# Norm stages in column halves, output stored in halves, and sixteen matmuls on a zeroed tile at the beginning

## The chip, the cores and the metric

The kernel runs on one core of a Trainium2 chip. The core has a matmul engine (TensorE, PE in the profile; its weight loads are listed apart as PEld), a vector engine (VectorE, DVE), an activation engine (ScalarE, ACT), a general engine (GpSimd, POOL) and a queue engine (SyncE, SP) that issues the DMA transfers here. Each engine works through its own list of instructions in order, and an instruction waits where it needs what another engine or a transfer has not finished. The metric is the time of one execution on the device in microseconds (us).

## The reference

The kernel computes four layers over 256 tokens of width 1024. Each layer is a half-step SwiGLU feed-forward network (FFN, inner width 2816), a token mixer with attention to 256 memory rows, and a second FFN. Each of the three takes a normed x and adds its normed result to x:

```python
def rms_norm(x, g):
    xf = x.astype(jnp.float32)
    y = xf * lax.rsqrt(jnp.mean(xf * xf, axis=-1, keepdims=True) + RMS_EPS)
    return (y * g.astype(jnp.float32)).astype(x.dtype)

def swiglu_ffn(x, w_gate_up, w_down):
    gate, up = jnp.split(x @ w_gate_up, 2, axis=-1)
    return (jax.nn.silu(gate) * up) @ w_down

for i in range(DEPTH):          # DEPTH = 4
    kind, j = i % 3, i // 3
    g = norm_g[i]
    x = x + 0.5 * rms_norm(swiglu_ffn(rms_norm(x, g[0]), ffn_w_gate_up[i, 0], ffn_w_down[i, 0]), g[1])
    h = rms_norm(x, g[2])
    mem_n = rms_norm(mem, mem_norm_g[i])
    y = ...                     # mixer A, B, C, A in layers 0 to 3, ends in a product with w_out
    x = x + rms_norm(y, g[3])
    x = x + 0.5 * rms_norm(swiglu_ffn(rms_norm(x, g[4]), ffn_w_gate_up[i, 1], ffn_w_down[i, 1]), g[5])
```

Between two of these parts stands what is called a norm boundary below: the result y of one part is normed and added to x, and x is normed for the next part. There are eleven such inner boundaries, one opening (only the norm of the input) and one end (only the norm of y, the addition and the store).

## The kernel before

**Layout.** x stays on the chip as two tiles (t = 0 and t = 1) of 128 tokens on partitions by 1024 columns, in float32. For the next part's matmuls the normed rows are transposed by TensorE in eight 128x128 blocks per tile, four to a PSUM tile of 512 columns (`rot`, four buffers).

**Three passes.** Every float32 product is made of three matmuls of operands split into a high and a low part (`mm3`, lines 334 to 336: hi by hi, hi by lo, lo by hi). A split is two instructions (`split`, lines 309 and 310): ScalarE copies the tile rounded into `hi`, VectorE subtracts that from the tile into `lo`. The weights stream in by SyncE's queue as units of 128x1024 (`raw`, five buffers) and are split into a ring of ten `hi` and `lo` buffers. A ring buffer comes free when TensorE has done the last matmul that reads it, and so ScalarE's `hi` can wait for TensorE. The same two lines split the transposed activations (`xth`, `xtl`); line 404 keeps a plain copy (`xf`) where an FFN follows, which works on two of its six column sets with a scheme of seven products in place of eight.

**A boundary.** `ln_stages` writes four stages for each tile t. s1: ScalarE squares the part's result in PSUM (`acc`, 128x1024) with the sum over columns as a by-product (line 374); VectorE multiplies the same result by the gain into `rows` (375); GpSimd makes 1/sqrt of the sum (348 adds epsilon, 349 takes the power). s2: VectorE adds rows times that factor to x (379). s3: ScalarE squares x (382), GpSimd as before. s4: VectorE makes the normed rows (386). `turn(t)` runs the four, `trans(t)` the eight transposes (400) with their splits.

**Order.** The two tiles are staggered. The last part's matmuls go tile 0 first (in `ffn`, `down(j, 0, ...)`, line 691 of the profile; in a mixer `out_step` with line 954). `turn(0)` follows, and TensorE meanwhile goes on with tile 1's matmuls; `trans(0)` stands inside the last but one of these (`late`, lines 747 and 961; after mixer B, ahead of all of them). Then comes `turn(1)`, and `trans(1)` inside the first products of the next part (line 584 in an FFN), or in the mixer's own beginning. Between these the calls of `slot` let the weight splits and loads of later units in. So the source gives an order; the framework's tile scheduler then merges all instructions, by its own estimates, into the list of each engine, and puts in the waits. In the program that results, weight splits of later units stand between the stages of a boundary, on ScalarE and on VectorE.

**Beginning and end.** `setup` loads x, the gain and the first five weight units, runs `turn(0)`, `trans(0)`, `turn(1)` and lets the weight splits begin; `first_set` of the first FFN is the first user. At the end, after the last `turn(1)`, two stores of 512 KB write x (line 753).

Of the kernel before, what the change touches and what calls it, by code (L numbers as in the profile page):

```python
# [18 lines left out]
P = 128  # L19
# [13 lines left out]
RING = 10  # L33
RAW = 5
HELD = 8
GRP = 4

def pairs(*cols):
# [165 lines left out]
class Trunk:  # L204
# [153 lines left out]
    def ln_stages(self, st, t, ps, post_scale, post_eps, gpost, gpre):  # L358
        nc = self.nc
        if "rows" not in st:  # L360
            st["rows"] = None
        ss = self.small.tile([P, 1], F32, tag="ss", name="ss", bufs=8)
        r = self.small.tile([P, 1], F32, tag="r", name="r", bufs=8)
        ss2 = self.small.tile([P, 1], F32, tag="ss2", name="ss2", bufs=8)
        r2 = self.small.tile([P, 1], F32, tag="r2", name="r2")
        x = self.x[t]

        def rows():
            if st["rows"] is None:
                st["rows"] = self.main.tile([P, 2, D], F32, tag="rows", name="rows")  # L370
            return st["rows"][:, t, :]

        def s1():
            nc.scalar.activation(out=self.dump(), in_=ps, func=AF.Square, scale=post_scale, accum_out=ss)  # L374
            nc.vector.tensor_tensor(out=rows(), in0=ps, in1=gpost, op=ALU.mult)  # L375
            self.rsqrt(r, ss, post_eps)

        def s2():
            nc.vector.scalar_tensor_tensor(out=x, in0=rows(), scalar=r, in1=x, op0=ALU.mult, op1=ALU.add)  # L379

        def s3():
            nc.scalar.activation(out=self.dump(), in_=x, func=AF.Square, scale=1 / 32, accum_out=ss2)
            self.rsqrt(r2, ss2, self.eps1)

        def s4():
            nc.vector.scalar_tensor_tensor(out=rows(), in0=x, scalar=r2, in1=gpre, op0=ALU.mult, op1=ALU.mult)

        out = []
        if ps is not None:
            out += [s1, s2]  # L390
        if gpre is not None:
            out += [s3, s4]
        return out
# [36 lines left out]
    def setup(self):  # L430
# [14 lines left out]
        nc.gpsimd.memset(self.neghalf, -0.5)  # L445
        nc.gpsimd.memset(self.eps1, EPS)
        nc.gpsimd.memset(self.eps16, 16 * EPS)
        turn = self.boundary(None, None, self.gpre)
        turn(0)
        self.trans(0, keep=self.keep)  # L450
# [83 lines left out]
    def ffn(self, l, f, post_next, pre_next, last=False):  # L534
        nc, tc = self.nc, self.tc
        with tc.tile_pool(name=f"ffn{l}{f}", bufs=1, reuse_waits="tile") as fp:
# [211 lines left out]
                down(j, 1, held[j - nd], (lambda: self.trans(0, keep=self.keep if f else None)) if late else None)  # L748
                self.slot(1)
            turn(1)  # L750
        if last:
            for t in range(2):
                nc.sync.dma_start(out=self.io["out"][t * P:(t + 1) * P, :], in_=self.x[t])

    def mem_chunk(self, k):
        m = self.main.tile([P, SEQ], F32, tag="snap", name="memraw", bufs=4)
# [585 lines left out]
```

## Time and profile before

| what | value |
|---|---|
| median of three runs | 1881.27 us (1877.97 to 1881.93) |
| profiled execution, its own time | 1876.93 us |
| span of that execution in the trace | 1875.1 us |
| TensorE busy (matmuls) | 1855.1 us, 99% of the span, 9406 instructions |
| TensorE weight loads, beside the matmuls | 1550.2 us, 83% |
| VectorE | 1517.5 us, 81% |
| ScalarE | 1092.6 us, 58% |
| GpSimd | 67.7 us, 4% |
| read from HBM | 359.95 MB, 193 GB/s over the span |

A row of a timeline reads: start in us from the beginning of the span, length in us, engine, line of the kernel, operation, what is written from what with their shapes, the count of instructions in the row (x8: eight in a row, and the length is of all of them together), and in brackets how long the engine had been idle before and what released it. Matmuls overlap, so one of 128x512 is listed with 0.39 us while the next starts after 0.227. Lines are those of the kernel before the change.

### The profile page before, as it was taken

How to read it: one execution, taken by the hardware profiler on the slowest of the kernel's cores; microseconds unless marked ns; L12 is line 12 of the kernel's file. 1: busy time of each engine (PE TensorE's matmuls, PEld its weight loads, DVE VectorE, ACT ScalarE, POOL GpSimd, SP SyncE). 2: the span in 40 equal slices, each digit the busy share in tenths (PEclk: the TensorE clock that was granted, in tenths of full speed). 3: DMA queues.
4: the chain of work that ended last, by engine and by line, in shares of the span. 5: the costliest groups of instructions: out<-in, count | busy, mean ns of one | idle time of the engine just before them, and what ended most of it. 6: DMA issues, size and time to landing. Idle time of an engine off the chain costs nothing.

```text
span 1875.1 us, 25124 instructions
## 1 busy us (share of the span) xinstructions
PE 1855.1 (99%) x9406; PEld 1550.2 (83%) x9406; DVE 1517.5 (81%) x1828; ACT 1092.6 (58%) x1471; POOL 67.7 (4%) x115
## 2 busy tenths in 40 slices
PE   8999999999999999999999999999999999999998
PEld 6888988888888897888888889888888888988886
DVE  7897879886888768888688876888868897878884
ACT  7556655755566555665556556465556555655652
POOL 0000200000000100000000000000000000200000
PEclk9999999999999999999999999999999999999999
DMA  8646737645574652664557366275477436737731
GB/s 321 237 154 212 261 124 257 232 161 193 177 247 135 215 198 91 247 226 155 191 192 247 124 205 237 91 254 173 146 246 241 167 124 210 263 124 254 243 101 60
DMA packets 103867, 362.67 MB, mean 193 GB/s; under 512 B 12084, under 2 KB 16576, under 8 KB 103616
## 3 DMA queue, kind: packets, MB, share of 16 engines
q1 hardware_dynamic: 103568, 359.47, 56.1%
q8 instruction: 74, 1.21, 0.3%
q0 software_dynamic: 176, 1.59, 0.2%
q14 instruction: 49, 0.40, 0.1%
HBM read 359.95 MB, written 1.06 MB: 193 GB/s over the span
## 4 chain that ended last, share of the span: by engine, by line
PE 88%; DVE 6%; issue 3%; ACT 1%; POOL 1%; DMA 1%; SPq 0%; ACTq 0%; DVEq 0%; POOLq 0%
PE acc L691 22%; PE rot L621 16%; PE rot L334 13%; PE rot L336 13%; PE rot L335 13%; PE acc L954 3%; DVE lo L310 3%; PE rot L562 2%; PE rot L856 1%; PE acc L874 1%; DMA raw<-in_w 1%; PE rot L888 1%; DVE x L379 1%; PE rot L400 1%; DVE rows L375 1%
## 5 line engine op out<-in xcount | busy, mean ns | idle before, releaser
L310 DVE TENSOR_TENSOR lo<-raw,hi 128x1024 fp32r<-128x1024 f32 (+1 forms) x515 | 620.2, 1220 | 142.9 <-ACT hi L309 135.2
L309 ACT ACTIVATE hi<-raw 128x1024 fp32r<-128x1024 f32 (+1 forms) x515 | 536.2, 1053 | 266.5 <-PE acc L691 84.1
L334 PE MATMUL rot<-hi,xth 128*128 128x512 f32 (+3 forms) x1072 | 415.2, 387 | 0.5 <-ACT hi L309 0.5
L336 PE MATMUL rot<-hi,xtl 128*128 128x512 f32 (+3 forms) x1072 | 412.2, 385 | 0.4 <-DVE xtl L310 0.3
L335 PE MATMUL rot<-lo,xth 128*128 128x512 f32 (+3 forms) x1072 | 411.6, 384 | 0.3 <-DVE lo L310 0.3
L309 ACT ACTIVATE hi<-quad 128x1024 fp32r<-128x1024 f32 x224 | 235.5, 1059 | 201.6 <-PE rot L336 129.2
L310 DVE TENSOR_TENSOR lo<-quad,hi 128x1024 fp32r<-128x1024 f32 x224 | 272.1, 1222 | 25.0 <-ACT hi L309 21.1
L336 PEld LDWEIGHTS rot<-hi,xtl 128*128 128x128 f32 x1072 | 201.7, 188 | 42.7 <-DVE xtl L310 4.0
L334 PEld LDWEIGHTS rot<-hi,xth 128*128 128x128 f32 x1072 | 201.8, 188 | 39.1 <-ACT hi L309 1.1
L335 PEld LDWEIGHTS rot<-lo,xth 128*128 128x128 f32 x1072 | 201.9, 188 | 38.8 <-DVE lo L310 0.7
L691 PE MATMUL acc<-hi,hh 128*128 128x512 f32 x640 | 197.9, 390 | 0.0
L691 PE MATMUL acc<-lo,hh 128*128 128x512 f32 x640 | 197.2, 389 | 0.0
L691 PE MATMUL acc<-hi,hl 128*128 128x512 f32 x640 | 197.1, 389 | 0.0
L621 PE MATMUL rot<-hi,sums 128*128 128x512 f32 x512 | 169.0, 396 | 0.1
L277 DVE TENSOR_TENSOR quad<-quad 128x1024 f32<-128x1024 f32 x128 | 154.8, 1220 | 1.2
L691 PEld LDWEIGHTS acc<-hi,hl 128*128 128x128 f32 x640 | 120.1, 188 | 25.2
L691 PEld LDWEIGHTS acc<-lo,hh 128*128 128x128 f32 x640 | 120.1, 188 | 25.1
L691 PEld LDWEIGHTS acc<-hi,hh 128*128 128x128 f32 x640 | 119.5, 188 | 24.3
L621 PEld LDWEIGHTS rot<-hi,sums 128*128 128x128 f32 x512 | 96.1, 188 | 24.3 <-DVE snap L641 4.8
L621 PE MATMUL rot<-lo,sums 128*128 128x512 f32 x256 | 99.8, 390 | 0.0
L348 POOL TENSOR_TENSOR r<-ss,thin 128x1 f32<-128x1 f32 x48 | 23.5, 490 | 1577.5 <-ACT junk L374 1484.7
L621 PE MATMUL rot<-hi,xtl 128*128 128x512 f32 x192 | 74.8, 389 | 0.0
(212 smaller groups left out, 2363.8 us busy)
## 6 DMA issues: line engine op xcount, KB each, us to landing
raw<-in_w SPq DMA_DIRECT2D x504, 512.0 KB, 4.5
quad<-in_w SPq DMA_DIRECT2D x128, 512.0 KB, 5.8
gpre<-in_norm_g SPq DMA_DIRECT2D x8, 512.0 KB, 5.6
gpost<-in_norm_g SPq DMA_DIRECT2D x8, 512.0 KB, 4.5
memraw<-in_mem_t SPq DMA_DIRECT2D x32, 128.0 KB, 4.3
g<-in_norm_g SPq DMA_DIRECT2D x8, 512.0 KB, 6.1
raw<-in_w SPq DMA_DIRECT2D x8, 384.0 KB, 3.7
sw<-in_sw SPq DMA_DIRECT2D x2, 768.0 KB, 9.0
```

The lines of the kernel that those rows point to most:

```text
L277: add = lambda x, y: self.nc.vector.tensor_tensor(out=x, in0=x, in1=y, op=ALU.add)
L309: self.nc.scalar.activation(out=hi, in_=src, func=AF.Copy)
L310: self.nc.vector.tensor_tensor(out=lo, in0=src, in1=hi.bitcast(F32), op=ALU.subtract)
L334: mm(out, a[0], b[0], start=start, stop=False)
L335: mm(out, a[0], b[1], start=False, stop=False)
L336: mm(out, a[1], b[0], start=False, stop=stop)
L348: g.tensor_tensor(out=out, in0=ss, in1=eps_tile, op=ALU.add)
L375: nc.vector.tensor_tensor(out=rows(), in0=ps, in1=gpost, op=ALU.mult)
L562: nc.tensor.transpose(ps[:, k * P:(k + 1) * P], T[s][t][:, k * P:(k + 1) * P], self.ident)
L621: nc.tensor.matmul(ps, a[i], w[j][:, kk, :], start=fresh and h == kk == i == j == 0, stop=h == kk == i == 1, skip_group_check=True)
L691: mm(ys[t][:, n * 512:(n + 1) * 512], x, y[:, 0, n * 512:(n + 1) * 512], start=(j == 0 and x is a[0] and y is w[0]), stop=(j == NF - 1 and ...
L954: self.nc.tensor.matmul(o["y"][t][:, h * 512:(h + 1) * 512], x, y[:, 0, h * 512:(h + 1) * 512], start=(j == 0 and x is a[0] and y is w[0]) ...
```

## The change

The edit is to the norm stages, to `setup` and to the stores. In s1 each tile's result is now worked on in two column halves of 512: ScalarE squares the first while VectorE multiplies the second by the gain, then each takes the other half. The two sums of squares are put together by one more addition on GpSimd. s2 is one instruction as before, but at the end of the program it is two halves, and each is stored as soon as it is there: four stores of 256 KB in place of two of 512 KB. s4 makes the normed rows in two halves, and so the first four transposes read only the first. s3 is unchanged. At the beginning VectorE zeroes a tile, and TensorE does 16 matmuls of 128x512 on it into a PSUM tile that nobody reads.

```diff
--- before.py
+++ after.py
@@ -33,6 +33,7 @@
 RING = 10
 RAW = 5
 HELD = 8
+WARM = 16
 GRP = 4
 
 def pairs(*cols):
@@ -359,11 +360,12 @@
         nc = self.nc
         if "rows" not in st:
             st["rows"] = None
-        ss = self.small.tile([P, 1], F32, tag="ss", name="ss", bufs=8)
+        ss = self.small.tile([P, 2], F32, tag="ss", name="ss", bufs=8)
         r = self.small.tile([P, 1], F32, tag="r", name="r", bufs=8)
         ss2 = self.small.tile([P, 1], F32, tag="ss2", name="ss2", bufs=8)
         r2 = self.small.tile([P, 1], F32, tag="r2", name="r2")
         x = self.x[t]
+        H = D // 2
 
         def rows():
             if st["rows"] is None:
@@ -371,19 +373,33 @@
             return st["rows"][:, t, :]
 
         def s1():
-            nc.scalar.activation(out=self.dump(), in_=ps, func=AF.Square, scale=post_scale, accum_out=ss)
-            nc.vector.tensor_tensor(out=rows(), in0=ps, in1=gpost, op=ALU.mult)
-            self.rsqrt(r, ss, post_eps)
+            dump = self.dump()
+            for a, b in ((0, 1), (1, 0)):
+                nc.scalar.activation(out=dump[:, a * H:a * H + H], in_=ps[:, a * H:a * H + H], func=AF.Square,
+                                     scale=post_scale, accum_out=ss[:, a:a + 1])
+                nc.vector.tensor_tensor(out=rows()[:, b * H:b * H + H], in0=ps[:, b * H:b * H + H],
+                                        in1=gpost[:, b * H:b * H + H], op=ALU.mult)
+            nc.gpsimd.tensor_tensor(out=r, in0=ss[:, 0:1], in1=post_eps, op=ALU.add)
+            self.rsqrt(r, ss[:, 1:2], r)
 
         def s2():
-            nc.vector.scalar_tensor_tensor(out=x, in0=rows(), scalar=r, in1=x, op0=ALU.mult, op1=ALU.add)
+            parts = 2 if gpre is None else 1
+            for i in range(parts):
+                h = slice(i * D // parts, (i + 1) * D // parts)
+                nc.vector.scalar_tensor_tensor(out=x[:, h], in0=rows()[:, h], scalar=r, in1=x[:, h], op0=ALU.mult,
+                                               op1=ALU.add)
+                if gpre is None:
+                    nc.sync.dma_start(out=self.io["out"][t * P:(t + 1) * P, h], in_=x[:, h])
 
         def s3():
             nc.scalar.activation(out=self.dump(), in_=x, func=AF.Square, scale=1 / 32, accum_out=ss2)
             self.rsqrt(r2, ss2, self.eps1)
 
         def s4():
-            nc.vector.scalar_tensor_tensor(out=rows(), in0=x, scalar=r2, in1=gpre, op0=ALU.mult, op1=ALU.mult)
+            for i in range(2):
+                h = slice(i * H, i * H + H)
+                nc.vector.scalar_tensor_tensor(out=rows()[:, h], in0=x[:, h], scalar=r2, in1=gpre[:, h], op0=ALU.mult,
+                                               op1=ALU.mult)
 
         out = []
         if ps is not None:
@@ -445,6 +461,11 @@
         nc.gpsimd.memset(self.neghalf, -0.5)
         nc.gpsimd.memset(self.eps1, EPS)
         nc.gpsimd.memset(self.eps16, 16 * EPS)
+        warm = self.dump()
+        nc.vector.memset(warm, 0.0)
+        ps = self.rot()
+        for _ in range(WARM):
+            nc.tensor.matmul(ps, warm[:, :P], warm[:, 512:], start=True, stop=True)
         turn = self.boundary(None, None, self.gpre)
         turn(0)
         self.trans(0, keep=self.keep)
@@ -748,9 +769,6 @@
                 down(j, 1, held[j - nd], (lambda: self.trans(0, keep=self.keep if f else None)) if late else None)
                 self.slot(1)
             turn(1)
-        if last:
-            for t in range(2):
-                nc.sync.dma_start(out=self.io["out"][t * P:(t + 1) * P, :], in_=self.x[t])
 
     def mem_chunk(self, k):
         m = self.main.tile([P, SEQ], F32, tag="snap", name="memraw", bufs=4)
```

In the changed kernel the lines are numbered up to 22 higher: the squares are L378 (before L374), the products L380 (L375), x is L389 (L379), its square L395 (L382), the rows L401 (L386), the transposes L416 (L400), weight splits L310 and L311 (L309 and L310), the mixer's output matmuls L972 (L954).

The merged lists of the engines differ by more than the diff says. First place: ScalarE, at the boundary out of the mixer of layer 0 into its second FFN, first tile. `acc` is the mixer's output in PSUM, `junk` a tile that nobody reads, `ss` the sum of squares, `hi` and `raw` the weight units; what stands behind "waits" is the engine or queue that the instruction waits for. Before:

```order
L374 ACTIVATE junk,ss<-acc 128x1024 [waits PE_49]
L309 ACTIVATE hi<-raw 128x1024 [waits DMAHW6_49,PE_49]
L309 ACTIVATE hi<-raw 128x1024 [waits DMAHW7_49,PE_49]
L382 ACTIVATE junk,ss_2530<-x_72 128x1024 [waits DVE_49]
L309 ACTIVATE hi<-raw 128x1024 [waits DMAHW0_49,PE_49]
```

and after the change:

```order
L378 ACTIVATE junk,ss<-acc 128x512 [waits PE_49]
L310 ACTIVATE hi<-raw 128x1024 [waits DMAHW6_49,PE_49]
L378 ACTIVATE junk,ss<-acc 128x512 [waits DVE_49]
L310 ACTIVATE hi<-raw 128x1024 [waits DMAHW7_49,PE_49]
L310 ACTIVATE hi<-raw 128x1024 [waits DMAHW0_49,PE_49]
L310 ACTIVATE hi<-raw 128x1024 [waits DMAHW2_49,PE_49]
L395 ACTIVATE junk,ss_2559<-x_72 128x1024 [waits DVE_49]
```

A weight split stands between the two squares, and four of them in place of two stand ahead of the square of x. The second square waits for VectorE.

VectorE at the same place, before:

```order
L375 TENSOR_TENSOR rows<-acc,g_1938 128x1024 [waits Activation_49]
L379 SCALAR_TENSOR_TENSOR x_72<-rows,r,x_72 128x1024 [waits DVE_49,Pool_49]
L310 TENSOR_TENSOR lo<-raw,hi 128x1024 [waits DMAHW6_49,Activation_49]
L310 TENSOR_TENSOR lo<-raw,hi 128x1024 [waits DMAHW7_49,Activation_49]
L386 SCALAR_TENSOR_TENSOR rows<-x_72,r_2531,g_1940 128x1024 [waits DVE_49,Pool_49]
```

and after the change:

```order
L380 TENSOR_TENSOR rows<-acc,g_1967 128x512 [waits Activation_49]
L311 TENSOR_TENSOR lo<-raw,hi 128x1024 [waits DMAHW6_49,Activation_49]
L380 TENSOR_TENSOR rows<-acc,g_1967 128x512 [waits Activation_49]
L311 TENSOR_TENSOR lo<-raw,hi 128x1024 [waits DMAHW7_49,Activation_49]
L389 SCALAR_TENSOR_TENSOR x_72<-rows,r,x_72 128x1024 [waits DVE_49,Pool_49]
L311 TENSOR_TENSOR lo<-raw,hi 128x1024 [waits DMAHW0_49,Activation_49]
L311 TENSOR_TENSOR lo<-raw,hi 128x1024 [waits DMAHW2_49,Activation_49]
L401 SCALAR_TENSOR_TENSOR rows<-x_72,r_2560,g_1969 128x512 [waits DVE_49,Pool_49]
L401 SCALAR_TENSOR_TENSOR rows<-x_72,r_2560,g_1969 128x512
```

Both halves of the product wait for ScalarE, a `lo` stands behind each of them ahead of x, and two more stand between x and the rows. Nine of the eleven inner boundaries look like this; those after mixers B and C have no weight split between the squares of the first tile.

Second place: TensorE at the same boundary, first tile's transposes (L400, L416) between the second tile's output matmuls, before:

```order
L954 MATMUL acc<-hi,mgh 128x512 x2
L400 MATMUL rot<-ident,rows 128x128 x8
L954 MATMUL acc<-lo,mgh 128x512 x2
L954 MATMUL acc<-hi,mgl 128x512 x2
L954 MATMUL acc<-hi,mgh 128x512 x2
L954 MATMUL acc<-lo,mgh 128x512 x2
L954 MATMUL acc<-hi,mgl 128x512 x2
```

and after the change:

```order
L972 MATMUL acc<-lo,mgh 128x512 x2
L972 MATMUL acc<-hi,mgl 128x512 x2
L972 MATMUL acc<-hi,mgh 128x512
L416 MATMUL rot<-ident,rows 128x128 x4
L972 MATMUL acc<-hi,mgh 128x512
L416 MATMUL rot<-ident,rows 128x128 x4
L972 MATMUL acc<-lo,mgh 128x512 x2
L972 MATMUL acc<-hi,mgl 128x512 x2
```

The transposes come five matmuls later, and one matmul stands between the two groups of four. The second tile's transposes keep their place.

Third place: VectorE at the program's beginning (`gpre` is the first gain, `T` the first product of the FFN). Before:

```order
L386 SCALAR_TENSOR_TENSOR rows<-x_72,r_97,gpre 128x1024
L310 TENSOR_TENSOR lo<-raw,hi 128x1024
L310 TENSOR_TENSOR xtl<-rot,xth 128x4x128
L310 TENSOR_TENSOR lo<-raw,hi 128x1024
L310 TENSOR_TENSOR xtl<-rot,xth 128x4x128
L310 TENSOR_TENSOR lo<-raw,hi 128x1024
L386 SCALAR_TENSOR_TENSOR rows<-x_73,r_127,gpre 128x1024
L310 TENSOR_TENSOR lo<-raw,hi 128x1024 x4
L543 SCALAR_TENSOR_TENSOR T<-T,rot 128x512
L310 TENSOR_TENSOR lo<-raw,hi 128x1024 x2
L310 TENSOR_TENSOR xtl<-rot,xth 128x4x128
```

and after the change:

```order
L465 MEMSET junk 128x512
L401 SCALAR_TENSOR_TENSOR rows<-x_72,r_116,gpre 128x512 x2
L311 TENSOR_TENSOR lo<-raw,hi 128x1024
L311 TENSOR_TENSOR xtl<-rot,xth 128x4x128 x2
L311 TENSOR_TENSOR lo<-raw,hi 128x1024
L401 SCALAR_TENSOR_TENSOR rows<-x_73,r_147,gpre 128x512 x2
L311 TENSOR_TENSOR lo<-raw,hi 128x1024 x5
L564 SCALAR_TENSOR_TENSOR T<-T,rot 128x512
L311 TENSOR_TENSOR lo<-raw,hi 128x1024 x3
L311 TENSOR_TENSOR xtl<-rot,xth 128x4x128 x2
```

The second tile's rows moved ahead of the third `lo`, and the second tile's xtl behind one more. On TensorE the second tile's transposes all stand 8 matmuls later than before.

## The prediction

> **What bounds the kernel now.** I read the page first, then TensorE's waits, then the timeline of one norm boundary, of the beginning and of the end.
>
> ```profile
> span 1875.1 us, 25124 instructions
> PE 1855.1 (99%) x9406; PEld 1550.2 (83%) x9406; DVE 1517.5 (81%) x1828; ACT 1092.6 (58%) x1471; POOL 67.7 (4%) x115
> ```
>
> TensorE is busy for 99% of the span, so only an edit that shortens or lengthens one of its waits moves the time. The list of who waited for whom, TensorE alone (sum in us, count, longest), names the largest that the change touches:
>
> ```profile
> PE rot L400 <- DVE rows L386: 10.3, 5, 8.2
> ```
>
> 8.2 us of that lie before the first transpose of the program; the other four are 0.5 us each, at transposes of the second token tile (128 tokens) of a norm boundary into an FFN, and a fifth of that kind stands under another name at 290.75 below. Beside the boundaries the change touches the cold beginning and the tail after the last matmul.
>
> **A boundary before, first tile** (out of the token mixer of layer 0 into its second FFN; timeline):
>
> ```profile
> 268.77 1.02 ACT L374 ACTIVATE junk<-acc 128x1024 bf16<-128x1024 f32 x1 [6.65 <-PE acc L954]
> 269.92 1.22 DVE L375 TENSOR_TENSOR rows<-acc,g 128x1024 f32<-128x1024 f32 x1 [7.33 <-ACT junk L374]
> 270.13 1.06 ACT L309 ACTIVATE hi<-raw 128x1024 fp32r<-128x1024 f32 x1 [0.25 <-PE acc L954]
> 271.26 1.28 DVE L379 SCALAR_TENSOR_TENSOR x<-rows,r,x 128x1024 f32<-128x1024 f32 x1
> 272.46 2.35 DVE L310 TENSOR_TENSOR lo<-raw,hi 128x1024 fp32r<-128x1024 f32 x2
> 272.58 1.06 ACT L382 ACTIVATE junk<-x 128x1024 bf16<-128x1024 f32 x1
> 273.63 3.00 ACT L309 ACTIVATE hi<-raw 128x1024 fp32r<-128x1024 f32 x3
> 273.80 1.05 POOL L348 TENSOR_TENSOR r<-ss,thin 128x1 f32<-128x1 f32 x1 [3.02 <-ACT junk L382]
> 274.94 0.55 POOL L349 TENSOR_TENSOR r<-r,thin 128x1 f32<-128x1 f32 x1
> 275.52 1.28 DVE L386 SCALAR_TENSOR_TENSOR rows<-x,r,g 128x1024 f32<-128x1024 f32 x1 [0.71 <-POOL r L349]
> ...
> 277.19 1.03 PE L400 MATMUL rot<-ident,rows 128*128 128x128 f32 x8
> ...
> 280.13 1.28 DVE L310 TENSOR_TENSOR xtl<-rot,xth 128x512 fp32r<-128x512 f32 x2
> ...
> 280.87 0.50 PE L336 MATMUL rot<-hi,xtl 128*128 128x512 f32 x1
> ```
>
> Three things are to be seen. VectorE's L375 starts after ScalarE's square, so nothing overlaps there today. The weight split `hi` at 270.13 idled 0.25 us for TensorE: its buffer came free only then. And GpSimd's add at 273.80 took 1.05 us and ended with the pair of `lo` (272.46 + 2.35 = 274.81); rows begin 0.71 us after that pair.
>
> Second tile of the same boundary:
>
> ```profile
> 285.86 1.28 DVE L379 SCALAR_TENSOR_TENSOR x<-rows,r,x 128x1024 f32<-128x1024 f32 x1
> 287.23 1.06 ACT L382 ACTIVATE junk<-x 128x1024 bf16<-128x1024 f32 x1 [3.23 <-DVE x L379]
> 288.46 0.19 POOL L348 TENSOR_TENSOR r<-ss,thin 128x1 f32<-128x1 f32 x1 [4.11 <-ACT junk L382]
> 289.31 1.28 DVE L386 SCALAR_TENSOR_TENSOR rows<-x,r,g 128x1024 f32<-128x1024 f32 x1 [2.17 <-POOL r L349]
> 289.84 0.39 PE L336 MATMUL rot<-hi,xtl 128*128 128x512 f32 x1
> 290.75 1.06 PE L400 MATMUL rot<-ident,rows 128*128 128x128 f32 x8 [0.52 <-DVE rt L510]
> ```
>
> And the `hi` at the last such boundary, in layer 3:
>
> ```profile
> 1675.94 1.06 ACT L309 ACTIVATE hi<-raw 128x1024 fp32r<-128x1024 f32 x1 [0.25 <-PE acc L954]
> ```
>
> TensorE could have gone on at 290.07 (289.84 plus one matmul interval of 0.227) and started at 290.75, 0.16 us after rows ended: 0.68 us lost. In layer 3 `hi` waited for the same 0.25 us.
>
> **The change, part by part.**
>
> *Halves on the first tile.* A half on VectorE takes 0.68 us and lets the next start after 0.60 (280.13: two end after 1.28); whole `lo` rows start 1.13 us apart (2.35 for two). A half square is not in the trace; I take 0.60, the length of this other half on ScalarE, plus 0.09 until the sum is out (the whole: 1.11 to its end in place of 1.02):
>
> ```profile
> L404 ACT ACTIVATE xf<-rot 128x512 f32<-128x512 f32 x32 | 19.0, 595 | 3.8 <-DVE xtl L310 3.7
> ```
>
> The order shows that the halves wait for each other in turn (square, product, square, product), and that in nine of the eleven inner boundaries a `hi` stands between the two squares and a `lo` after each product. From 268.77: square 269.45, product 270.17. `hi` cannot start before its buffer is free at 270.13, so ScalarE reaches the second square at 271.10, out at 271.78; before, the whole sum was out at 269.88. VectorE goes on with `lo` (behind that `hi`) 271.22 to 272.44, the second product to 273.03, `lo` of the second `hi` to 274.17, then x at 274.08 in place of 271.26: 2.8 us late. Square of x 275.40, sum out 276.55; the two `lo` behind x end at 277.63, GpSimd's add, issued at 276.6 during the second, is held to their end as at 273.80, and rows start at 277.63 + 0.71 = 278.34. First half done at 279.02, second at 279.62.
>
> TensorE meets its transposes five matmuls later than before, 277.19 + 5 x 0.227 = 278.32, and can start at 279.02 + 0.16 = 279.18. It loses 0.86 us. The second four find their half ready. It gets about 0.2 back, because before it then waited for xtl (the row at 280.87 is 0.50 long in place of 0.39). Net **0.66 us**. Bounds: if GpSimd is not held, rows start 0.7 earlier and the loss is 0; if the given-back part is lost again, 0.86.
>
> The Trainium skill's page "SBUF — State Buffer" (Who interferes with whom) says that a VectorE instruction with two SBUF inputs blocks a GpSimd instruction that reads SBUF; `lo` has two. By that rule the loss is the 0.66 above, without it 0; the rows at 273.80 (1.05 us beside `lo`) and 288.46 (0.19 us beside none) are on its side.
>
> *Where that loss stays.* In the four boundaries into a mixer the second tile's transposes come microseconds after their rows, so the loss stays: 3 x 0.66, and 0.66 + 0.45 in layer 2, where the transposes moved back three matmuls and not five (2 x 0.227 less time). **+3.1 us** (0.5 to 4.5).
>
> *Second tile, five boundaries into an FFN.* Here TensorE's own wait of 0.68 absorbs a shift, but the chain moves too. After the first tile's rows (279.62) VectorE now does a `lo`, two xtl and two `lo` (1.13 + 1.20 + 2.26), so the first product starts at 284.21. In turn follow the square, meanwhile a `lo`, and the second product from 285.94 to 286.62; GpSimd is held by that `lo`, and r is out when the product is. x starts at 286.65 in place of 285.86, and what follows is 0.79 late: the first half of rows ends at 290.78 and its transposes run from 290.94 to 291.47, those of the second, from 290.78 + 0.60 + 0.16 = 291.54, to 292.07. Before, all eight ended at 290.75 + 1.06 = 291.81. The 0.6 that the first half gains is less than what was lost: **+0.25 each, +1.25** (-2.2 to +3.5). The two remaining boundaries (after mixers B and C) have no `hi` of that kind between their squares: 0.
>
> *Beginning.*
>
> ```profile
> 10.41 1.06 ACT L309 ACTIVATE hi<-raw 128x1024 fp32r<-128x1024 f32 x1 [0.48 <-DMA raw<-in_w]
> 11.54 0.63 PE L334 MATMUL rot<-hi,xth 128*128 128x512 f32 x1
> 13.89 0.39 PE L334 MATMUL rot<-hi,xth 128*128 128x512 f32 x1
> 15.93 1.28 DVE L386 SCALAR_TENSOR_TENSOR rows<-x,r,gpre 128x1024 f32<-128x1024 f32 x1 [1.29 <-POOL r L349]
> 18.41 0.50 PE L335 MATMUL rot<-lo,xth 128*128 128x512 f32 x1 [0.30 <-DVE lo L310]
> 24.07 1.06 ACT L309 ACTIVATE hi<-raw 128x1024 fp32r<-128x1024 f32 x1 [1.28 <-DMA raw<-in_w]
> 25.06 0.39 PE L336 MATMUL rot<-hi,xtl 128*128 128x512 f32 x1
> ```
>
> The first matmuls are slow (0.63) and from 13.6 us fast (0.39). The 16 new ones take between 16 x 0.227 = 3.6 and, at the slow spacing of about 0.42, 6.7 us (counted from the starts between these two rows); started with the program, they are over before the first rows are ready, for which TensorE waited 8.2 us. They cost nothing and may warm the clock. But TensorE then waits for VectorE: the second tile's rows now stand before the third `lo`. The square for them follows `hi` (10.41) and two xf of 0.6, and its sum is out at 13.7; with 0.9 through GpSimd (288.38, when the sum of the square at 287.23 was out, to 289.31), rows take 14.63 to 15.83, in place of 15.93 to 17.2, and five `lo` follow, ending at 17.05, 18.2, 19.3 and so on. At 17.1 TensorE has done 13 of the first pass's 48 matmuls and no second-tile transpose: 35 x 0.227 + 1.06 = 9.0, so the pass ends at 26.1; before, at 25.06 + 0.23 = 25.3. The xtl of the second tile now stands behind the `lo` of the weights landing at 24.07, and is ready at 26.8, 0.3 after its turn. **+1.1 us** (0.4 to 1.7). The halves of x's product (0.68 twice in place of 1.28) are in this.
>
> *End.*
>
> ```profile
> 1867.63 1.02 ACT L374 ACTIVATE junk<-acc 128x1024 bf16<-128x1024 f32 x1 [9.77 <-PE acc L691]
> 1868.78 1.22 DVE L375 TENSOR_TENSOR rows<-acc,gpost 128x1024 f32<-128x1024 f32 x1 [8.26 <-ACT junk L374]
> 1870.12 1.28 DVE L379 SCALAR_TENSOR_TENSOR x<-rows,r,x 128x1024 f32<-128x1024 f32 x1
> 1871.43 0.34 SPq L753 DMA_DIRECT2D out_x<-x  x1
> ```
>
> The list of DMA issues gives the two stores 2.6 us from issue to landing:
>
> ```profile
> out_x<-x SPq DMA_DIRECT2D x2, 512.0 KB, 2.6
> ```
>
> In turn, the four halves take 4 x 0.68 plus handovers of 0.04: second product done at 1870.47, r at 1870.66 (0.9 through GpSimd after the second sum), x halves end at 1871.38 and 1871.98. The last store is issued 0.58 later than the whole was, but carries half: if none of the 2.6 us goes with the size that is +0.6, if all does -0.7. I take the middle, **-0.05 us**.
>
> Sum: 3.1 + 1.25 + 1.1 - 0.05 = **+5.4 us**. The profiled execution took 1876.93 (1875.1 of span and 1.8 around it) and lies 4.3 below the median of the runs, 1881.27; both were the same program, so I add the sum to the median: **1886.7 us**, 0.29% slower. About 0.2% (3.8 us) can be told from no change.
>
> **Rivals.**
>
> *GpSimd is not held.* Then x's second square is followed by rows 0.7 earlier: nothing is lost on the first tile (0.45 in layer 2), the second tile ends 0.45 earlier than before, five times: 0.45 - 2.25 + 1.1 - 0.05 = -0.75, **1880.5**. Against it stands the row at 273.80. It decides if the adds that follow x on a first tile take 0.2 us.
>
> *Halves pay on the second tile.* If `hi` between the squares does not hold the chain (no wait for its buffer) and x starts at 285.86 as now, the first half's transposes fill the wait: 5 x -0.6 = -3.0, no first-tile loss, 1.1 at the beginning, -0.05 at the end: -1.95, **1879.3**, not slower. Against it: the 0.25 us wait at 270.13 and 1675.94. It decides when x of the second tile is no more than 0.1 later.
>
> *The beginning is a matter of TensorE's clock.* 16 matmuls at 0.42 in place of 0.227 cost 3.1 us; if that, and not VectorE, sets the beginning, the term is -3.1 in place of +1.1, and the sum +1.2: **1882.5**. For it: rows 11.54 and 13.89. Against it: TensorE's wait for `lo` at 18.41. The Trainium skill's page "TensorE: Matmul & The Clock Gate" (Part 1) has this as a rule: half rate until some 3.4 us of sustained work, which the added matmuls would supply.
>
> **Chances.** Forecast 0.60 (above the bound of 1885.0 in 0.46, below in 0.14); GpSimd free 0.16, within; halves pay 0.12 (0.07 within, 0.05 faster); clock 0.12 (0.08 within, 0.04 faster). Faster 0.09, within 0.45, slower 0.46. The bounds of the terms add up to between -2.0 and +10.3 us, seldom all at once; the range 1878.5 to 1890.5 takes in every rival.
>
> **What would show it.** Right: in nine boundaries over 2 us between the two squares of a first tile, x some 5.3 us after the first square, TensorE waiting 0.6 to 1 us at its transposes; first-pass matmuls 0.39 long from the start, then a stop until about 17 us; the last store issued about 0.6 us later after the last matmul than before, and landed about when it did. Wrong: squares of one tile within 1.5 us, or first-tile transposes without a wait, or the matmul after the first pass before 25.3.

## The result and the profile after

The changed kernel takes 1889.76 us (median of four runs, 1889.03 to 1890.73) beside 1879.77 us of the kernel before (four runs, 1877.97 to 1881.93): the ratio is 1.0053, with a 95% interval of 1.0036 to 1.0070. It is slower by about 10 us. A second comparison on another occasion gave 1.0051 (1.0038 to 1.0064). The forecast was +5.4 us, 1886.7: the right side, and half of the size.

The page of the changed kernel begins:

```profile
span 1888.2 us, 25313 instructions
PE 1862.1 (99%) x9422; PEld 1550.6 (82%) x9422; DVE 1524.5 (81%) x1879; ACT 1099.2 (58%) x1519; POOL 71.1 (4%) x139
```

and its list of TensorE's waits (sum, count, longest):

```profile
PE rot L416 <- DVE rows L401: 9.9, 15, 1.2
PE rot L336 <- DVE lo L311: 2.8, 3, 2.0
PE rot L468 <- DVE junk L465: 1.5, 1, 1.5
PE rot L583 <- DVE T L749: 1.4, 3, 0.5
```

Before, the transposes waited for rows five times, and 8.2 of 10.3 us of that lay at the cold start. Now they wait fifteen times. The longest wait, 1.2 us, is the program's first, behind the 16 matmuls; the other fourteen lie at boundaries, and ten of them at first tiles, which did not wait before. To see where the 13.1 us between the two spans arose, I set matmul number n of one trace beside number n of the other (without the 16 new ones) and read how far it had fallen behind at each place. The same sum is made for every kernel below; "boundaries" are the stretches of 30 matmuls ahead of a first tile's transposes to 30 behind the second's, "beginning" ends at 100 us, "rest" is all else.

| kernel | beginning | boundaries | end | rest | span against before |
|---|---|---|---|---|---|
| forecast for the change | +1.1 | +4.35 | -0.05 | 0 | +5.4 |
| changed kernel | +2.6 | +7.9 | +0.35 | +2.2 | +13.1 |
| changed kernel, second profile | +2.5 | +7.8 | +0.35 | +0.2 | +10.9 |

I do not count the rest as the change's: two profiles of the same changed kernel have 2.2 and 0.2 of it. It is made of waits for `T` ahead of the boundaries into mixers and of waits inside mixers. Its size differs from -1.5 to +3.3 us between profiles. Kernels that leave s1 alone have it too, and the one profile of the kernel before (1876.93 us) lies 0.9 to 1.6 us below the medians of its 15 to 27 runs in the later comparisons (1877.8 to 1878.6). Where I followed one of these waits back, in layer 2, it came from a load of the memory's rows. Before and after:

```profile
1094.85 0.51 ACT L768 ACTIVATE mgh<-memraw,thin 128x256 fp32r<-128x256 f32 x1 [2.39 <-DMA memraw<-in_mem_t]
```

```profile
1103.28 0.51 ACT L786 ACTIVATE mgh<-memraw,thin 128x256 fp32r<-128x256 f32 x1 [3.20 <-DMA memraw<-in_mem_t]
```

TensorE is 7.9 us behind there, the load 8.43: half a microsecond that shows at the next transposes of `T`.

**A boundary after** (out of the mixer of layer 0, the one that the prediction worked through), first tile:

```profile
272.91 0.60 ACT L378 ACTIVATE junk<-acc 128x512 bf16<-128x512 f32 x1 [6.63 <-PE acc L972]
273.63 0.69 DVE L380 TENSOR_TENSOR rows<-acc,g 128x512 f32<-128x512 f32 x1 [6.89 <-ACT junk L378]
274.27 1.06 ACT L310 ACTIVATE hi<-raw 128x1024 fp32r<-128x1024 f32 x1 [0.67 <-PE acc L972]
275.24 0.58 ACT L378 ACTIVATE junk<-acc 128x512 bf16<-128x512 f32 x1
276.50 0.68 DVE L380 TENSOR_TENSOR rows<-acc,g 128x512 f32<-128x512 f32 x1
278.24 1.28 DVE L389 SCALAR_TENSOR_TENSOR x<-rows,r,x 128x1024 f32<-128x1024 f32 x1
279.44 2.35 DVE L311 TENSOR_TENSOR lo<-raw,hi 128x1024 fp32r<-128x1024 f32 x2
280.78 1.06 POOL L349 TENSOR_TENSOR r<-ss,thin 128x1 f32<-128x1 f32 x1 [3.52 <-ACT junk L395]
282.50 1.41 DVE L401 SCALAR_TENSOR_TENSOR rows<-x,r,g 128x512 f32<-128x512 f32 x2 [0.71 <-POOL r L350]
283.31 0.66 PE L416 MATMUL rot<-ident,rows 128*128 128x128 f32 x4 [0.69 <-DVE rows L401]
```

ScalarE's second square starts 2.33 us after its first: between them it waits 0.67 us for a ring buffer and then splits a weight unit. x starts 5.33 us after the first square (2.49 before), rows 9.59 us (6.75 before), and the transposes wait.

Second tile of the same boundary, and behind it, for the length of the pass, one row of the kernel before:

```profile
288.44 0.68 DVE L380 TENSOR_TENSOR rows<-acc,g 128x512 f32<-128x512 f32 x1
289.98 0.32 POOL L349 TENSOR_TENSOR r<-ss,r 128x1 f32<-128x1 f32 x1 [1.42 <-ACT junk L378]
290.96 1.28 DVE L389 SCALAR_TENSOR_TENSOR x<-rows,r,x 128x1024 f32<-128x1024 f32 x1
294.42 1.42 DVE L401 SCALAR_TENSOR_TENSOR rows<-x,r,g 128x512 f32<-128x512 f32 x2 [2.18 <-POOL r L350]
295.32 1.29 PE L416 MATMUL rot<-ident,rows 128*128 128x128 f32 x8 [0.19 <-DVE rows L401]
296.37 0.48 PE L335 MATMUL rot<-hi,xth 128*128 128x512 f32 x1
```

```profile
291.57 0.48 PE L334 MATMUL rot<-hi,xth 128*128 128x512 f32 x1
```

The first matmul behind the transposes stands 23.46 us after the boundary's first square, and 291.57 - 268.77 = 22.80 before: 0.66 us lost at this boundary in all. The eight transposes now take 1.05 us to the next matmul in place of 0.82, since the second four wait for their half.

**The beginning after:**

```profile
9.74 0.49 PE L335 MATMUL rot<-hi,xth 128*128 128x512 f32 x1 [0.83 <-ACT xth L310]
14.66 0.50 PE L335 MATMUL rot<-hi,xth 128*128 128x512 f32 x1 [0.26 <-ACT hi L310]
15.93 5.76 DVE L311 TENSOR_TENSOR lo<-raw,hi 128x1024 fp32r<-128x1024 f32 x5
17.20 0.50 PE L336 MATMUL rot<-lo,xth 128*128 128x512 f32 x1 [2.04 <-DVE lo L311]
17.78 0.63 PE L335 MATMUL rot<-hi,xth 128*128 128x512 f32 x1
21.18 0.39 PE L337 MATMUL rot<-hi,xtl 128*128 128x512 f32 x1
24.86 1.06 ACT L310 ACTIVATE hi<-raw 128x1024 fp32r<-128x1024 f32 x1 [0.75 <-DMA raw<-in_w]
```

The first pass starts at the full rate, as the 16 matmuls could bring about, and then stops from 14.66 to 17.20 behind the second tile's rows and a `lo`. Eight matmuls behind the stop are slow again.

**The end after:**

```profile
1879.68 0.61 PE L712 MATMUL acc<-hi,el 128*128 128x512 f32 x2
1882.50 0.69 DVE L380 TENSOR_TENSOR rows<-acc,gpost 128x512 f32<-128x512 f32 x1 [0.75 <-ACT junk L378]
1883.46 1.42 DVE L389 SCALAR_TENSOR_TENSOR x<-rows,r,x 128x512 f32<-128x512 f32 x2 [0.27 <-POOL r L350]
1884.24 0.99 SPq L392 DMA_DIRECT2D out_x<-x  x2
```

```profile
out_x<-x SPq DMA_DIRECT2D x4, 256.0 KB, 2.0
```

Before, the last pair of matmuls was

```profile
1866.98 0.61 PE L691 MATMUL acc<-hi,el 128*128 128x512 f32 x2
```

x is finished 5.20 us after the start of the last pair (1884.88), before the change 4.42 (1871.40): 0.8 later. A store lands in 2.0 us (median of four) in place of 2.6.

### The profile page after: what moved, and what is told of

Read it like the earlier page. It is cut to its first block, busy times and chain, and to the rows that moved or that the text cites. A ratio compares the mean times of both kernels' runs of the same rounds, so it can differ in the third digit from the quotient of the medians.

```text
span 1888.2 us, 25313 instructions
## 1 busy us (share of the span) xinstructions
PE 1862.1 (99%) x9422; PEld 1550.6 (82%) x9422; DVE 1524.5 (81%) x1879; ACT 1099.2 (58%) x1519; POOL 71.1 (4%) x139
## 3 DMA queue, kind: packets, MB, share of 16 engines
HBM read 359.95 MB, written 1.06 MB: 191 GB/s over the span
## 4 chain that ended last, share of the span: by engine, by line
PE 83%; DVE 7%; DMA 4%; ACT 3%; issue 2%; POOL 2%; SPq 0%; DVEq 0%; ACTq 0%; POOLq 0%
PE acc L712 21%; PE rot L642 15%; PE rot L335 13%; PE rot L336 13%; PE rot L337 13%; DVE lo L311 3%; PE acc L972 3%; DMA memraw<-in_mem_t 2%; PE rot L583 2%; DMA raw<-in_w 2%; ACT hi L310 1%; PE rot L874 1%; PE rot L416 1%; PE acc L892 1%; PE rot L906 1%
## 5 line engine op out<-in xcount | busy, mean ns | idle before, releaser
L311 DVE TENSOR_TENSOR lo<-raw,hi 128x1024 fp32r<-128x1024 f32 (+1 forms) x515 | 624.3, 1224 | 151.9 <-ACT hi L310 144.3
L310 ACT ACTIVATE hi<-raw 128x1024 fp32r<-128x1024 f32 (+1 forms) x515 | 535.7, 1052 | 266.5 <-PE acc L712 88.3
L310 ACT ACTIVATE hi<-quad 128x1024 fp32r<-128x1024 f32 x224 | 235.5, 1059 | 201.0 <-PE rot L337 131.8
L311 DVE TENSOR_TENSOR lo<-quad,hi 128x1024 fp32r<-128x1024 f32 x224 | 272.3, 1222 | 24.2 <-ACT hi L310 20.2
L378 ACT ACTIVATE junk<-acc 128x512 bf16<-128x512 f32 x48 | 28.5, 594 | 94.6 <-PE acc L712 53.8
```

What stands on the lines that cost most here:

```text
L310: self.nc.scalar.activation(out=hi, in_=src, func=AF.Copy)
L311: self.nc.vector.tensor_tensor(out=lo, in0=src, in1=hi.bitcast(F32), op=ALU.subtract)
L378: nc.scalar.activation(out=dump[:, a * H:a * H + H], in_=ps[:, a * H:a * H + H], func=AF.Square, scale=post_scale, accum_out=ss[:, a:a + 1])
```

## The experiments

All were timed beside the kernel before. Differences are between medians; the intervals are those of the ratio. The last columns are read from each kernel's trace as above.

| kernel | difference, us | ratio (95%) | beginning | boundaries | end | rest |
|---|---|---|---|---|---|---|
| e1: s1 in turn, both tiles | +12.8 | 1.0070 (1.0056 to 1.0083) | +0.3 | +13.2 | +0.7 | -1.5 |
| e9: s1 in turn, first tile | +9.3 | 1.0050 (1.0037 to 1.0062) | +0.7 | +9.6 | 0 | +0.3 |
| e7: s1 in turn, second tile | +2.6 | 1.0014 (1.0005 to 1.0023) | 0 | +2.0 | +0.7 | +0.6 |
| e4: squares halved, not in turn | +3.0 | 1.0014 (1.0005 to 1.0023) | +0.7 | +3.2 | +0.2 | +1.9 |
| e2: all but s1 | +3.1 | 1.0018 (1.0009 to 1.0027) | +2.4 | +0.55 | -0.3 | +3.3 |
| e12: s4 and stores | +2.8 | 1.0015 (1.0006 to 1.0024) | +1.6 | +0.55 | -0.3 | +1.25 |
| e6: 16 matmuls alone | +2.7 | 1.0014 (1.0006 to 1.0023) | +2.6 | 0 | 0 | +1.8 |
| e3: all but the 16 matmuls | +9.4 | 1.0049 (1.0036 to 1.0061) | +1.6 | +8.2 | +0.3 | +0.6 |
| e5: the whole change again | +9.8 | 1.0051 (1.0038 to 1.0064) | +2.5 | +7.8 | +0.35 | +0.2 |
| e10: whole, transposes later | +6.6 | 1.0036 (1.0024 to 1.0049) | +2.4 | +5.6 | +0.35 | -0.5 |
| e8: before, transposes later | -2.5 | 0.9987 (0.9978 to 0.9996) | +0.2 | -2.9 | 0 | +1.9 |
| e11: e8 and stores in halves | -3.1 | 0.9982 (0.9973 to 0.9991) | +0.2 | -2.8 | -0.3 | +0.9 |

**e1: s1 alone.** Only s1 (and the two-column `ss`) of the diff is put into the kernel before.

```diff
-            nc.scalar.activation(out=self.dump(), in_=ps, func=AF.Square, ...)
-            nc.vector.tensor_tensor(out=rows(), in0=ps, in1=gpost, op=ALU.mult)
+            for a, b in ((0, 1), (1, 0)):
+                nc.scalar.activation(... half a ...)
+                nc.vector.tensor_tensor(... half b ...)
```

> The kernel before with only s1 in halves in turn (no warm matmuls, s4 and the stores whole). Theory A (the turn of square and product lets weight splits in ahead of x, and this delays the rows of both tiles): the order again has hi between the squares and lo behind each product; x of the first tile about 2.8 us late, TensorE waits 0.7 to 0.9 us at nine first-tile transposes, and the second tile's wait at the boundaries into an FFN grows from 0.68 to about 1.6 us, since no half of rows comes early: +8 to +12 us over the kernel before, as much as the whole change or more. Theory B (the loss is at the beginning and in the halves of s4): not more than +3 us. The first 30 us of the program are as before by both.

Measured +12.8 us, more than the whole change; the beginning is as before. In TensorE's list of waits:

```profile
PE rot L406 <- DVE rows L392: 17.4, 16, 8.2
PE rot L336 <- DVE xtl L310: 3.1, 8, 0.9
```

9.2 us of waits for rows lie outside the cold start, and eight waits for xtl (3.1 us) come on top, where before there was one of 0.3. Theory A holds, B falls. That s1 alone costs 13.2 us at the boundaries and the whole change 7.9 says that s4's halves, with the order that they bring, win 5 us, but only back from the loss that s1 makes.

**e9 and e7: which tile.** s1 is in turn on one tile and whole on the other.

```diff
-            (the loop over the halves)
+            if t == 0:        # e9; t == 1 in e7
+                (the loop over the halves)
+            else:
+                (square and product whole)
```

> s1 in halves in turn on the first tile only; the second tile, the rest and the beginning as before. Theory A (the first tile's turn, with hi between the squares and a lo behind each product, is nearly the whole loss of s1): 0.7 to 0.8 us lost at a first tile's transposes, 0.4 to 1 us more at its xtl, 0.6 to 0.9 us at the second tile's transposes before an FFN, which inherit the delay; +9 to +12 us. Theory E (both tiles share the loss about equally): +5 to +7 us.

> s1 in halves in turn on the second tile only; the first tile, the rest and the beginning as before. Theory A (most of the loss is the first tile's: x 2.8 us late there, and the second tile inherits it): first tiles lose nothing, x of the second tile is 0.2 to 0.6 us later before an FFN: +1 to +3 us. Theory E (the second tile's own turn is what costs): +5 us or more.

+9.3 and +2.6 us: the first tile has nearly the whole loss. At its transposes TensorE loses 0.7 to 0.8 us, and 0.44 to 0.95 at eight xtl behind them (one of these waited before, too); at the second tile's transposes before an FFN it waits only 0.2 in place of 0.68. A late first tile uses up the slack of the second. The two boundary terms, 9.6 and 2.0, add up to 11.6 of the 13.2 that both have together. I expected 0.6 to 0.9 at that last place, which was wrong.

**e4: squares halved, but not in turn.**

```diff
+            for a in range(2):
+                nc.scalar.activation(... half a, accum_out=ss[:, a:a + 1])
+            nc.vector.tensor_tensor(out=rows(), in0=ps, in1=gpost, op=ALU.mult)
```

> The kernel before with only the square of s1 in two halves one behind the other, then the product whole (nothing in turn, no weight split between the squares), GpSimd's extra add kept. One lo stands ahead of x where before there was none. Theory A1 (what counts is the lo ahead of x, by whatever way it got there): x of the first tile 1.2 us late, rows 1.1 us late at an unmoved place of the transposes: TensorE loses about 0.7 us at a first tile, +5 to +8 us. Theory A2 (the wait in turn, with hi between the squares, is what counts): +0 to +2 us.

+3.0 us, between the two. x is 1.1 us later than before, as A1 had it (1.2), and TensorE loses 0.67 to 0.91 us at nine first tiles. But a boundary into an FFN loses only 0.14 to 0.2 net, because the second tile's wait falls from 0.68 to 0.14 to 0.2. A1 was right on the stall and wrong on the price: it forgot the slack that follows. In turn a like stall costs 0.6 and more at these places: in e9 the second tile's wait falls too, but a wait for xtl of 0.44 or more stands behind the transposes, and in e1 and the whole change the second tile's chain is late as well.

**e2: all but s1.** The changed kernel with s1 as before.

> The whole change except s1, which is as before. Theory A: boundaries keep their order, first tiles wait nowhere, the second tile's wait of 0.68 us before an FFN shrinks to about 0.4, so the boundaries gain 1 to 2 us; the beginning still loses 2.5 us (VectorE's order, and the clock that falls back in the stop), the end gains or loses under 0.4: within 2 us of the kernel before. Theory B: +5 us or more, most of the loss of the change.

+3.1 us, of which the trace puts 2.4 at the beginning and 0.55 at boundaries; a gain of 1 to 2 us from s4's halves was expected there and is not. The timeline of the second tile shows why:

```profile
285.44 3.48 DVE L310 TENSOR_TENSOR lo<-raw,hi 128x1024 fp32r<-128x1024 f32 x3
288.84 1.22 DVE L376 TENSOR_TENSOR rows<-acc,g 128x1024 f32<-128x1024 f32 x1
290.16 1.28 DVE L383 SCALAR_TENSOR_TENSOR x<-rows,r,x 128x1024 f32<-128x1024 f32 x1
```

Three `lo` stand ahead of the product where before stood two with one behind it. With the 3.98 us that TensorE is behind at the start of this boundary, x is 0.32 us late (290.16 - 3.98 - 285.86), and TensorE waits 0.31 us for the first half and 0.2 for the second in place of 0.68 for the whole. The gain of the half went into the order.

**e6, e3 and e12: the 16 matmuls.** e6 has them alone, e3 is the changed kernel without them, e12 has s4 and the stores in halves alone (e2 without them).

```diff
+        warm = self.dump()
+        nc.vector.memset(warm, 0.0)
+        ps = self.rot()
+        for _ in range(16):
+            nc.tensor.matmul(ps, warm[:, :P], warm[:, 512:], start=True, stop=True)
```

> The kernel before with the memset and the 16 matmuls alone. The order of every boundary is as before, but at the beginning the second tile's rows stand ahead of a lo and all eight of its transposes come later, as in the whole change. Theory A (order sets the beginning): the first pass runs fast and then stops for 2 us or more until about 17.5 us; +1 to +3 us. Theory C (a warm TensorE pays): -1.5 to -3 us.

> The whole change without the memset and the 16 matmuls. Theory A (the stop of 2 us in the first pass is set by VectorE's rows and lo, and TensorE's rate falls back in it): TensorE's first matmuls are slow again, 0.63 us long, but the matmul behind the stop still starts near 17.2 us and the slow rows behind it come as well; so within 1 us of the whole change. Theory C (the matmuls pay): 1.5 to 3 us slower than the whole change. Theory D (the matmuls and their order cost the beginning): 2 to 3 us faster than the whole change.

> s4 and the stores in halves, s1 as before and no matmuls at the beginning: the kernel with all but s1, less the memset and the 16 matmuls. Its order at the beginning differs from that one by a third lo that stands ahead of the second tile's xtl there and not here. Theory D (the matmuls cost, by the order they bring about): 0.9 to 1.3 us less lost in the first 60 us than with them (about +1.2 in place of +2.3 in the trace), +1 to +2.5 us over the kernel before. Theory C (they pay): more lost than with them, +4 us or more.

They do not pay. Alone they cost 2.7 us, all of it at the beginning (theory A). Without them the halves lose 1.6 us there, with them 2.4 to 2.6, and the medians of e3 and of the whole change differ by 0.4 us, less than their ranges. e12 came out at +2.8, a little above what was expected, with 1.6 at the beginning. VectorE's list shows a difference that fits: e12 does the second tile's xtl behind one `lo` of a late load,

```profile
24.60 1.22 DVE L310 TENSOR_TENSOR lo<-raw,hi 128x1024 fp32r<-128x1024 f32 x1 [0.66 <-ACT hi L309]
25.74 1.29 DVE L310 TENSOR_TENSOR xtl<-rot,xth 128x512 fp32r<-128x512 f32 x2
```

and the whole change (here its second profile) behind two:

```profile
24.13 1.23 DVE L311 TENSOR_TENSOR lo<-raw,hi 128x1024 fp32r<-128x1024 f32 x1 [0.71 <-ACT hi L310]
26.12 1.23 DVE L311 TENSOR_TENSOR lo<-raw,hi 128x1024 fp32r<-128x1024 f32 x1 [0.77 <-ACT hi L310]
27.27 1.28 DVE L311 TENSOR_TENSOR xtl<-rot,xth 128x512 fp32r<-128x512 f32 x2
28.00 0.50 PE L337 MATMUL rot<-hi,xtl 128*128 128x512 f32 x1 [0.65 <-DVE xtl L311]
```

**e5: the whole change once more**, unedited.

> The changed kernel once more, beside the same runs of the kernel before as the next three. Theory A: +9 to +12 us, with the same waits at the transposes (0.85 to 0.95 us at first tiles, 0.3 and 0.28 at second ones). Two things of its first profile are on trial: the slow matmuls behind the stop of the beginning (0.63 us long from 17.8 to 21.2 us), which would return if the length of the stop alone decided, but which two kernels with a like stop did not show; and the waits of 0.5 us for T ahead of three boundaries into mixers, which also stood in kernels without s1 in halves: if loads set them, they differ from profile to profile.

+9.8 us, and the waits at the transposes are the same to 0.1 us. The slow matmuls behind the stop did not come back, although the stop was as long (14.66 to 17.20); TensorE then waited 0.32 us for xth and 0.65 for xtl, and the beginning cost the same 2.5 us. So the slow matmuls cost nothing here: they filled a time in which TensorE otherwise waited for ScalarE and VectorE. The waits for `T` were two in place of three, and e1 had none.

**e8, e10 and e11: a cheaper way to the same wait.** In every FFN but the first, the second tile's transposes move from ahead of the last six matmuls of a pass into their middle.

```diff
-                        pair(held[4 + i], u, i, t)
-                        ...
-                        if t == 0 and i == 2:
-                            self.trans(1, keep=self.keep)
+                        here = t == 0 and i == 3 and (l, f) != (0, 0)
+                        pair(held[4 + i], u, i, t, (lambda: self.trans(1, keep=self.keep)) if here else None)
```

where `pair` calls its last argument after its first three matmuls. e8 is the kernel before with this, e10 the changed kernel with it, e11 is e8 with the change's s2 (two halves, four stores).

> Not a part of the change: the kernel before with the second tile's transposes three matmuls (0.68 us) later in the first pass of every FFN but the first, nothing else. If the wait of 0.68 us at five boundaries is all that a shorter norm chain could win, this wins it without touching the norm: the wait vanishes, xth and xtl still come in time, -2 to -3.4 us. If the wait only moves to the matmuls behind the transposes: within 1 us.

> The whole change, and the second tile's transposes of every FFN but the first three matmuls later. If TensorE's waits at the second tile (0.3 and 0.28 us at five boundaries, 1.27 and 0.28 after mixer C) are what is left of the second tile's late chain, they shrink to nothing at five boundaries and to about 0.9 at one: 3 to 4 us faster than the whole change, +6 to +7 us over the kernel before. The waits of 0.85 to 0.95 us at the first tiles stay. If the delay moves on to the matmuls behind: within 1.5 us of the whole change.

> The kernel before with the second tile's transposes three matmuls later, and the last addition and the stores in halves (s2 of the change; s1, s4 and the beginning as before). The end is 0.3 us shorter, as in the kernel with all but s1, the boundaries 2.9 us: -2.5 to -3.5 us against the kernel before, if nothing else moves.

e8 is faster than the kernel before by 2.5 us (0.9978 to 0.9996). Its only wait for rows is the cold start:

```profile
PE rot L400 <- DVE rows L386: 8.2, 1, 8.2
```

Five boundaries gain 0.57 to 0.61 us each, 2.9 in all. e10 is 3.2 us faster than the whole change was (+6.6 against +9.8), with the first tiles' waits unchanged. e11 is the fastest kernel of the study, 3.1 us faster than the kernel before (0.9973 to 0.9991) and 13 us faster than the changed one by the differences to the kernel before.

## Why the prediction was right on the side and short on the size

The range, 1878.5 to 1890.5, holds the measured 1889.76 partly by luck. The sum was added to a median of 1881.27, which stood 1.5 us above that of the comparison (1879.77), and the trace puts more on the change (2.6 + 7.9 + 0.35 = 10.85 us) than the bounds of the terms allowed (10.3).

**The chain of the first tile: right.** From the first square to x 5.33 us (forecast 274.08 - 268.77 = 5.31), to rows 9.59 (9.57), to the transposes 10.40 (10.41). At that last step two small errors cancelled: a half of rows took 0.75 us and not 0.68, and the transposes followed it by 0.06 and not 0.16. TensorE lost 0.85 to 0.94 us there at every boundary of this order (0.86). e1, e9 and e4 show that the cause is the turn on the first tile: e9 alone makes 9.6 of the 13.2 us.

**Boundaries into a mixer: right.** +3.1 forecast, 0.43 + 0.81 + 0.63 + 0.77 = 2.6 in the first profile. The 1.11 for layer 2 was too much (0.63): TensorE lost 0.94 at its first tile like the others and not 0.45 more.

**Second tile before an FFN: mis-sized.** The step "+0.25 each" measured 0.59 to 0.69, 3.2 in place of 1.25. The errors are small ones on a chain that ends last. x stood 18.05 us after the first square and not at 17.88: the first product came 0.09 us late (15.53 after the first square, forecast 15.44), and x started 0.11 after the second product had ended, where the sum allowed 0.03. Before the change it was 0.12 (269.92 + 1.22 to 271.26). Then the halves of rows were taken at 0.68 us, with the next 0.60 later, which is what halves of xtl take; they took 0.75 and 0.67, two of them 1.42 us at 294.42. The transposes followed each half by 0.15 us, as they followed the whole before. So the first four started at 22.41 after the first square (forecast 22.17), the second four another 0.07 late, and four took 0.63 us to their end, where the sum had 0.53. Here 0.4 us on a chain counts five times.

**After mixers B and C: wrong.** The step "have no `hi` of that kind between their squares: 0" measured 0.47 and 1.64 us. It looked for weight splits between the first tile's squares only. After B, x came 3.84 us behind the first square in place of 3.09 all the same, with a copy (`bpt`) between the two halves on VectorE. After C, first the row before, then three of after:

```profile
1233.84 2.35 DVE L310 TENSOR_TENSOR lo<-raw,hi 128x1024 fp32r<-128x1024 f32 x2
```

```profile
1242.56 3.49 DVE L311 TENSOR_TENSOR lo<-raw,hi 128x1024 fp32r<-128x1024 f32 x3
1246.68 0.60 ACT L420 ACTIVATE xf<-rot 128x512 f32<-128x512 f32 x1 [0.64 <-DVE xtl L311]
1248.12 1.06 ACT L310 ACTIVATE hi<-raw 128x1024 fp32r<-128x1024 f32 x1 [0.84 <-DMA raw<-in_w]
```

VectorE's order has three `lo` ahead of the first tile's xtl in place of two, and ScalarE's second-tile square started 2.6 us late: its xf waited 0.64 us for xtl, and a `hi` ahead of it waited 0.84 us for its load. The second tile's turn added its own delay.

**Beginning: mis-sized.** The stop came where it was forecast, to 17.20 (17.1). But the step "xtl ... ready at 26.8, 0.3 after its turn" took the load of the last weights at its old time, 24.07. Its `hi` started at 24.86 in the first profile and 25.03 in the second. A raw buffer comes free only with its `lo`: each weight load is issued about 0.03 us behind the end of one. The third `lo` now ended behind the second tile's rows, at 17.15 in place of 14.65, and the eighth load was issued at 17.18 in place of 14.67. The two loads behind it were issued when they were before (the last at 19.45, before at 19.52) and landed later. In the second profile TensorE was 0.87 us behind up to there, as forecast (26.1 - 25.3 = 0.8), and then lost 1.5 us for xth and xtl in place of 0.3; in the first, the slow matmuls took the place of that wait. So it was +2.5 to 2.6 in place of +1.1, above the bound of 1.7, and e3 and e12, which lose 1.6 without the 16 matmuls, show that these make about 1 us of it.

**End: mis-sized.** +0.35 in place of -0.05. In turn cost 0.7 (e1, e7), the halves of the store won 0.3 (e2, e11). The second product ended 3.51 us after the start of the last pair of matmuls (forecast 3.49); the halves of x ended at 5.20, forecast 5.00, which is half of the difference of 0.4: here, too, two halves took 1.42 us in place of 1.28. A store of half the size landed 0.6 us sooner, close to the middle that was taken; what the last of the four stores took alone the list does not show.

**Rivals.** That GpSimd is not held fell: its add beside two `lo` took 1.06 us at 280.78, as before, and 0.19 beside none (at 293.57). The rule of the Trainium skill's page "SBUF — State Buffer" (Who interferes with whom), by which a VectorE instruction with two SBUF inputs contends with a GpSimd instruction that reads SBUF, agrees with both rows. That the halves pay on the second tile fell too: x came there 0.96 us later than before (18.05 after the first square, 17.09 before), and in e2 and e7 the halves did not pay even without the turn on the first tile. That the beginning is a matter of TensorE's clock fell with e6: its first pass ran fast from 9.78 (matmuls 0.39 to 0.50 us long, 0.63 before), and the kernel was slower.

## What to carry to other kernels

Before splitting a step to overlap two engines, ask whether the two halves have to wait for each other, and what else is queued into the gaps that the split opens. Here each handover let a weight split of over a microsecond in, and four short steps became a chain 2.8 us longer. Look first at where the bound engine waits, and whether it can be given other work there: moving eight transposes by three matmuls won what halving the norm could not. Price a change of a scheduled program from its order as it comes out, for both tiles and for every boundary.

## What the hardware showed

TensorE's rate fell near the stop of the first pass in some profiles, not in all. In the changed kernel the row of the window view from 17.5 to 23 us (length, TensorE busy and count, granted clock, DMA share, GB/s) reads

```profile
17.50:23.00 5.50, 5.50 (x18) 0.69 0.70 233
```

and in its second profile, after the same stop of 2.5 us,

```profile
17.50:23.00 5.50, 5.50 (x26) 1.00 0.83 249
```

The slow stretch lasted 21.18 - 17.78 = 3.4 us at about half rate (eight matmuls, 0.425 us apart and not 0.227). Of the five profiles of kernels with the 16 matmuls, three had a window between 13 and 23 us with a clock of 0.69 or 0.70 (the changed kernel, e6, e10), two had none (e5, e2); nor had any of the nine kernels without them. It was not always behind the stop: in e6 the slow matmuls began at 18.61, 1.5 us after its end (17.11), and in e10 they began at 12.22, ahead of its stop (15.33 to 17.27) and with no idle time over 0.85 us since the 16 matmuls. The row of e10:

```profile
13.00:17.50 4.50, 3.09 (x7) 0.70 0.72 271
```

The Trainium skill's page "TensorE: Matmul & The Clock Gate" (Part 1) has the rate fall after an idle window of about 3.4 us and rise after as long a busy one. The 3.4 us of slow matmuls agree with it; a fall behind a stop of 2.5 us, or with no stop as in e10, does not follow from it. What decides between the profiles stays open. In the kernel before, the first matmuls were as slow (0.63 us) while the granted clock read 1.00, so that column does not show the cold start.
